# Five experts kept on chip in place of three, Y loaded three pieces sooner, and a last expert of 32 slots

## The chip, the cores and the metric

The kernel runs on one core of one Trainium2 chip. Its time is device microseconds of one execution; before the change the median of 3 runs is 979.84 us (975.59 to 984.9). The engines of the core are PE (TensorE, matmuls), VectorE (DVE in the rows), ScalarE (ACT), GpSimd (POOL) and SyncE (SP). Loads and stores are issued on SyncE's queue in program order; gathers and scatters by row index are issued by POOL.

## What is computed

One block over 512 tokens of width 1024: a convolution branch and a gated spatial branch, mixed and projected, then a mixture of 32 experts in 4 groups, and a last RMS norm. The part that the change touches is the end:

```python
e_w = jax.nn.softmax(top_v, axis=-1) * g_w          # two experts for each token
def run_block(args):
    xb, e = args
    return (jax.nn.silu(xb @ w_gate[e]) * (xb @ w_up[e])) @ w_down[e]
...
x = x + hierarchical_moe(h, ...)                    # sum of the two experts' rows, weighted
return rms_norm(x, norm_final_g)
```

Each expert has weights of 3 x 2 MB (gate and up in two halves of the contraction, and down), 201 MB in all, in float32. 512 tokens with two experts each make 1024 assignments.

## The kernel before

**Order of the experts.** The experts are ranked by their number of tokens (`kr`), except that ranks 0 to 2 are three fixed experts, whose weights can be loaded before the routing is known. Ranks 3 to 7 get 128 slots ("b"), 8 to 17 get 64 ("s"), 18 to 31 get 32 ("t"); ranks 0 to 2 also 64. The string `ORDER` (line 24) says in which order these are run, after the three fixed ones. In this text "expert n" is the n-th in that order, 0 to 31, and not a rank. Before, experts 27 to 31 are "s".

**The stream of weights.** `loads` (lines 772 to 776) lists the pieces in order of loading: (n, 0) and (n, 1) are the two halves of gate and up of expert n, (n, 2) its down weights, 2 MB each; (n - 1, 2) comes behind (n, 1). ("Y", 0) and ("Y", 1) are pieces too, 2 MB each. `piece()` (line 809) issues the next one on SyncE's queue; a weight piece waits until the piece two before it in turn has landed (`DEEP`, `throttle`), and each waits until its tile is free. There are nine tiles of 2 MB used in turn; one of them leaves the turn when ("late", 0) comes and holds tables from then on. The last expert's pieces are cut in 2, 4 and 4 DMAs. A DMA that waits holds up everything behind it on SyncE's queue.

**One expert.** POOL gathers its token rows; PE transposes them (`x_tr`, line 949). `up` (lines 967 and 971) makes gate and up, `glu` (978, 983) the product on ScalarE and VectorE, `h_tr` (990, 992) its transposes, and `down` (1001, 1013) the output. Experts of 64 slots run two column groups of 64 on PE, those of 32 slots four groups of 32. The main loop is software pipelined: `up(n, 0)`, `up(n, 1)`, `glu(n)`, `x_tr(n + 1)`, `down(n - 1)`, `h_tr(n)`. The program is scheduled by hand: each engine runs in the order in which the code is written.

**Where outputs go.** The output rows of experts 0 to 28 are scattered by POOL to the DRAM buffer `yd` (lines 1017 and 1039); its two halves, the first and the second choice of each token, are loaded as Y0 and Y1 (line 821), weighted and added to X by VectorE (`y_add`, line 1130). Y0's load waits for the scatters, and `scattered` (line 1156) holds it back in the program until they are issued. The last `NLATE` = 3 experts are not scattered. Experts 29 and 30 leave their rows side by side in one tile `LT["c"]` (`late_down`), and `late_add` multiplies it with a one-hot matrix that holds the weights (`late_oh`), so that PE puts each row at its token, and VectorE adds it to X (lines 1123 and 1125, 8 matmuls and 8 additions).

**The end.** The last expert's tokens get their whole row of X on PE as well: its slots' rows of X are picked by matmuls with `LT["ot"]` (`late_x`, line 1180) into the accumulator in which its down matmuls add (1001). For the other rows `finish_a` (1134, squares), `rsqrt` and `finish_b` (1138, product; 1139, store) make the final norm. The last expert's rows are normed at lines 1200 to 1204 and scattered over the output at line 1205.

Of the kernel before, what the change touches and what calls it, by code (L numbers as in the profile page):

```python
# [10 lines left out]
I32 = mybir.dt.int32  # L11
# [10 lines left out]
NS, NBIG, DEEP, NLATE, LATE_AT = 3, 8, 2, 3, -16  # L22
NOV, NMID = 15, 18
ORDER = "tsb" * 5 + "t" * 9 + "s" * 5
# [57 lines left out]
def body(tc, nc, d, out, dbg=None):  # L82
# [692 lines left out]
    loads = loads[:-3] + [(NE - 2, 2), ("Y", 0), ("Y", 1)] + [(NE - 1, q) for q in range(3)]  # L775
# [272 lines left out]
    sv, so = kt_([2, 2], "sv"), kt_([1], "so", I32)  # L1048
    mx, over = kt_([1], "mx"), kt_([1], "over", I32)

    def route_rest():
        for q in range(NLATE):
            r, h = order[NE - NLATE + q], (slice(0, 64), slice(64, 128), slice(0, 128))[q]
            dve.tensor_copy(sv[h, q // 2, 0:1], tb1[h, r:r + 1])
        dve.tensor_scalar(sv[:, :, 1], sv[:, :, 0], -float(T), None, ALU.add)
        dve.tensor_scalar(so, gi[:, order[-1]:order[-1] + 1], 2.0, hf01, ALU.mult, ALU.add)
# [16 lines left out]
        dve.tensor_tensor(same.rearrange("p (q s) -> p q s", q=2), ident[:, :64].unsqueeze(1).to_broadcast([128, 2, 64]),  # L1073
                          ident[:, 64:].unsqueeze(1).to_broadcast([128, 2, 64]), ALU.add)

    def late():
# [3 lines left out]
        LT["oh"] = t[:, D:D + T]  # L1080
# [13 lines left out]
    def late_oh(q):  # L1094
        last = q == 1
        oh = LT["tm"] if last else LT["oh"]
# [47 lines left out]
    for n in range(NE - 1):  # L1144
# [222 lines left out]
```

## Time and profile before

| | |
|---|---|
| median of 3 runs | 979.84 us (975.59 to 984.9) |
| profiled execution, its own time | 978.58 us |
| its span | 976.7 us |
| PE, VectorE, ScalarE, POOL busy | 88%, 42%, 22%, 10% of the span |
| data moved by DMA | 270.18 MB |

The execution shown in the rows below is the profiled one. The span runs from the first to the last instruction of the program; the time of an execution is some 1.9 us longer here. Matmuls in float32 have two records each in the trace, so 8 matmuls stand as x16.

### The profile page before, as it was taken

Reading aid. Unit: us, or ns where it says so; the run is one execution under the profiler, and the core shown is the slowest. Engines: PE = TensorE matmul, PEld = TensorE weight load, DVE = VectorE, ACT = ScalarE, POOL = GpSimd, SP = SyncE. Lnnn points to the kernel's source line nnn. Section 1 sums busy time; section 2 is a strip of 40 time slices with the busy share of each in tenths; the row PEclk is TensorE's granted clock in tenths of the full one; section 3 lists DMA queues with packets and bytes.
Section 4 is the critical chain, followed back from the end, with each engine's and each line's share of the span. In section 5 each row is a group of like instructions: output and inputs, shape, how many; then the busy total and the mean of one; then the engine's idle time right before and its main releaser. Section 6 shows DMA issues by size and latency. Waiting matters only on the chain.

```text
span 976.7 us, 11811 instructions
## 1 busy us (share of the span) xinstructions
PE 855.3 (88%) x4774; PEld 542.3 (56%) x4774; DVE 408.4 (42%) x715; ACT 219.0 (22%) x317; POOL 98.2 (10%) x97
## 2 busy tenths in 40 slices
PE   8999899999999999997599999797978765667883
PEld 6886578888877888886234443343433332322231
DVE  7796958888987633426401110010101000003063
ACT  6221222433216623233211101010101000001022
POOL 2220000000000000320211111010101111100000
PEclk9999999999999999999799999899999677789997
DMA  6538422222222232697599999999999999999994
GB/s 229 194 101 287 136 81 87 87 87 87 87 87 87 86 117 99 260 407 289 197 395 397 415 422 407 387 416 401 403 405 416 411 419 406 413 406 427 430 414 184
DMA packets 36253, 270.18 MB, mean 277 GB/s; under 512 B 7044, under 2 KB 9864, under 8 KB 19682
## 3 DMA queue, kind: packets, MB, share of 16 engines
q1 hardware_dynamic: 30912, 259.09, 66.8%
q0 software_dynamic: 5280, 10.28, 2.9%
q8 instruction: 39, 0.64, 0.3%
q14 instruction: 20, 0.16, 0.1%
q10 hardware_dynamic: 2, 0.00, 0.0%
HBM read 258.56 MB, written 15.73 MB: 281 GB/s over the span
## 4 chain that ended last, share of the span: by engine, by line
PE 44%; DMA 40%; DVE 8%; issue 3%; ACT 2%; SPq 1%; POOL 1%; POOLq 0%; DVEq 0%; ACTq 0%
DMA w<-in_wexp 37%; PE acc L357 22%; PE acc L365 7%; PE acc L971 7%; DVE cv L347 3%; PE acc L1001 3%; DMA f<-in_wmix 2%; DVE hl L169 1%; PE acc L336 1%; POOL hl L171 1%; ACT hl L158 1%; PE acc L967 1%; PE aux L478 1%; SPq L329 1%; PE acc L669 1%
## 5 line engine op out<-in xcount | busy, mean ns | idle before, releaser
L357 PE MATMUL acc<-hT,hl 128*128 128x512 f32 x912 | 211.7, 392 | 0.0
L971 PE MATMUL acc<-w,xT 128*64 128x512 f32 (+1 forms) x576 | 173.5, 620 | 23.8 <-DMA w<-in_wexp 22.9
L357 PEld LDWEIGHTS acc<-hT,hl 128*128 128x128 f32 x912 | 171.5, 189 | 37.0 <-issue 1.8
L983 DVE TENSOR_TENSOR h<-sg,acc 64x256 f32<-64x256 f32 (+2 forms) x31 | 17.4, 560 | 363.8 <-ACT sg L978 268.4
L971 PEld LDWEIGHTS acc<-w,xT 128*64 128x64 f32 (+1 forms) x576 | 61.3, 158 | 122.1 <-issue 101.7
L347 DVE SCALAR_TENSOR_TENSOR cv<-cv,cs,cv 128x500 f32<-128x500 f32 (+16 forms) x180 | 124.9, 752 | 0.6
L169 DVE TENSOR_TENSOR hl<-f,hl 128x2048 fp32r<-128x2048 f32 (+1 forms) x36 | 80.4, 2234 | 60.5 <-ACT hl L158 60.4
L967 PE MATMUL acc<-w,xT 128*32 128x256 f32 x896 | 66.2, 451 | 32.5 <-DMA w<-in_wexp 32.5
L1001 PE MATMUL acc<-w,hh 128*64 128x512 f32 (+1 forms) x288 | 83.1, 598 | 7.9 <-DMA w<-in_wexp 6.1
L158 ACT ACTIVATE hl<-f 128x2048 fp32r<-128x2048 f32 x35 | 66.8, 1912 | 61.2 <-issue 29.2
L978 ACT ACTIVATE sg<-acc 64x256 f32<-64x256 f32 (+2 forms) x32 | 16.0, 501 | 259.0 <-PE acc L971 167.1
L967 PEld LDWEIGHTS acc<-w,xT 128*32 128x32 f32 x896 | 32.0, 126 | 60.4 <-issue 24.9
L1001 PEld LDWEIGHTS acc<-w,hh 128*64 128x64 f32 (+1 forms) x288 | 29.2, 151 | 47.8 <-issue 41.1
L889 POOL DMA_INDIRECT xg<-h2d,gi x32 | 30.6, 956 | 234.4 <-PE aux L949 226.8
L1013 PE MATMUL acc<-w,hh 128*32 128x256 f32 x448 | 34.7, 463 | 17.5 <-DMA w<-in_wexp 17.5
L365 PE MATMUL acc<-hl,mT 128*128 128x512 f32 x192 | 47.0, 396 | 0.0
L614 POOL TENSOR_TENSOR X<-X,rbo 128x1024 f32<-128x1024 f32 x4 | 9.4, 2395 | 350.6 <-DVE hl L169 350.6
L357 PE MATMUL acc<-yT,hl 128*128 128x512 f32 x192 | 44.2, 389 | 0.0
L357 PE MATMUL acc<-sT,hl 128*128 128x512 f32 x192 | 44.2, 389 | 0.0
L365 PE MATMUL acc<-hl,hT 128*128 128x512 f32 x192 | 43.8, 390 | 0.0
L365 PEld LDWEIGHTS acc<-hl,hT 128*128 128x128 f32 x192 | 36.0, 188 | 8.3 <-issue 0.8
L357 PEld LDWEIGHTS acc<-sT,hl 128*128 128x128 f32 x192 | 36.1, 188 | 7.5
(274 smaller groups left out, 711.6 us busy)
## 6 DMA issues: line engine op xcount, KB each, us to landing
w<-in_wexp SPq DMA_DIRECT2D x93, 2048.0 KB, 10.5
f<-in_wmix SPq DMA_DIRECT2D x36, 1024.0 KB, 4.8
yd<-z SPq DMA_DIRECT2D x1, 4096.0 KB, 13.5
w<-yd SPq DMA_DIRECT2D x2, 2048.0 KB, 13.9
w<-in_wexp SPq DMA_DIRECT2D x8, 512.0 KB, 10.9
xs<-in_x SPq DMA_DIRECT2D x4, 512.0 KB, 5.9
X<-in_x SPq DMA_DIRECT2D x4, 512.0 KB, 6.1
h2d<-h POOLq DMA_DIRECT2D x4, 512.0 KB, 7.5
```

What stands on the lines that cost most here:

```text
L158: act.activation(HI[i], src, AF.Copy)
L169: dve.tensor_tensor(LO[i][:, :n], src[:, :n], h[:, :n], ALU.subtract)
L347: dve.scalar_tensor_tensor(cY[:, j, s_:], cA[:, j, :T - s_], cw(j, t), cY[:, j, s_:], ALU.mult, ALU.add)
L357: pe.matmul(p, w[:, k], mv[m][:, k], start=n == 0, stop=n == 3 * KT - 1)
L365: pe.matmul(p, mv[m][:, kh * 4 + k, bs], w[:, k], start=kh + n == 0, stop=kh == 1 and n == 11)
L889: pool.indirect_dma_start(out=XG[n % len(XG)][:m], out_offset=None, in_=h2d, in_offset=bass.IndirectOffsetOnAxis(ap=gi[:m, r:r + 1], axis= ...
L967: pe.matmul(E[n]["p"][i * 32:i * 32 + 32, :256], XT[n][:, kt], w[:, 1 - i // 2, kk, f:f + 256], start=kt == 0, stop=kt == KT - 1, skip_gro ...
L971: pe.matmul(E[n]["gu"[q]], XT[n][:, kt], w[:, q, kk], start=kt == 0, stop=kt == KT - 1, skip_group_check=True)
L978: act.activation(s_, E[n]["g"], AF.Silu)
L983: dve.tensor_tensor(h, s_, E[n]["u"], ALU.mult)
L1001: pe.matmul(y[hf], E[n]["hT"][:, kt], w[:, kt, hf * 512:hf * 512 + 512], start=first and kt == 0, stop=kt == 3, skip_group_check=True)
L1013: pe.matmul(p[i * 32:i * 32 + 32, :256], E[n]["hT"][:, kt % 2, f:f + 32], w[:, kt, i * 256:i * 256 + 256], start=kt == 0, stop=kt == 3, sk ...
```

## The change

`ORDER` puts one "t" behind the five "s", so that experts 26 to 30 have 64 slots and expert 31 has 32. `NLATE` becomes 5: experts 27 and 28 are kept in one tile, 29 and 30 in another, and `pair_add` adds each pair to X; the scatters end with expert 26. The tables for this need another one-hot matrix and are made two iterations sooner (`LATE_AT`, `late_rows`, `late_oh`). The Y pieces stand ahead of (30, 0). The eight Y additions move into the loop's last iteration, and the first pair's additions into the last two. The last expert runs in four groups of 32 slots, with 256 columns each, its X rows are taken between the two halves of `up`, and its output rows are scattered in quarters of a row.

```diff
-NS, NBIG, DEEP, NLATE, LATE_AT = 3, 8, 2, 3, -16
+NS, NBIG, DEEP, NLATE, LATE_AT = 3, 8, 2, 5, -22
-ORDER = "tsb" * 5 + "t" * 9 + "s" * 5
+ORDER = "tsb" * 5 + "t" * 8 + "s" * 5 + "t"
...
-    loads = loads[:-3] + [(NE - 2, 2), ("Y", 0), ("Y", 1)] + [(NE - 1, q) for q in range(3)]
+    loads = loads[:-3] + [(NE - 2, 2)] + [(NE - 1, q) for q in range(3)]
+    loads[-7:-7] = [("Y", 0), ("Y", 1)]
     loads.insert(LATE_AT, ("late", 0))
...
     def late_down(n, y):
-        if n == NE - NLATE:
-            LT["c"] = m1.tile([128, 2, DE], F32, name="yc", tag="ysb", bufs=2)
+        q, i = divmod(n - NE + NLATE, 2)
+        if i == 0:
+            LT["c", q] = m1.tile([128, 2, DE], F32, name="yc", tag="ysb", bufs=2)
...
+    def pair_add(q, bs=range(NB)):
+        for b in bs:
+            late_add([LT["oh"][:, q]] * 2, [LT["c", q][:, hf] for hf in range(2)], b)
+
+    def last_down(p, first):
+        w = W[NE - 1, 2].rearrange("p (k f) -> p k f", k=4)
+        for kt in range(4):
+            f = kt // 2 * 32
+            for i in range(4):
+                pe.matmul(p[i * 32:i * 32 + 32, :256], E[NE - 1]["hT"][:, kt % 2, f:f + 32], w[:, kt, i * 256:i * 256 + 256],
+                          start=first and kt == 0, stop=kt == 3, skip_group_check=True)
...
         x_tr(n + 1)
+        if n == NE - 2:
+            Y = [W["Y", j] for j in range(2)]
+            for b in range(NB):
+                y_add(Y, 0, [b])
+                y_add(Y, 1, [b])
         if n:
             down(n - 1)
+            if n == NE - NLATE:
+                scattered.append(True)
             piece()
-        if n == NE - NLATE:
-            scattered.append(True)
         h_tr(n)
...
+        if n in (NE - 3, NE - 2):
+            pair_add(0, (0, 1) if n == NE - 3 else (2, 3))
...
     down(NE - 2)
-    for b in range(NB):
-        y_add(Y, 0, [b])
-        late_add([LT["oh"]] * 2, [LT["c"][:, hf] for hf in range(2)], b)
...
+    for b in range(NB):
+        pair_add(1, (b,))
+        finish_a(O, [b])
+    rsqrt(fs[:, 1], fs[:, 0], fs[:, 2], 1.0 / D)
+    act.activation(f1[:, 0:1], eps, AF.Silu)
+    up(NE - 1, 0)
...
+    p = acc()
+    for b in range(NB):
+        for i in range(4):
+            pe.matmul(p[i * 32:i * 32 + 32, :256], LT["ot"][:, b, :32], X2[:, b, i * 256:i * 256 + 256], start=b == 0,
+                      stop=False, skip_group_check=True)
+    up(NE - 1, 1)
+    finish_b(O, (0, 1))
+    glu(NE - 1)
+    h_tr(NE - 1)
+    finish_b(O, (2, 3))
+    act.activation(f1[:, 0:1], eps, AF.Sqrt)
+    last_down(p, False)
```

On SyncE's queue, the loads near the end before (`w92` is (29, 2), `w93` is (30, 2), `w94` and `w95` are Y0 and Y1, `w96` the first half of expert 31; the number behind a w is the place in the list of pieces):

```order
L836 DMA w92_5509<-in_wexp 128x4096
L836 ISA
L836 DMA w93_5519<-in_wexp 128x4096
L821 DMA w94_5631<-yd_75 128x4x1024
L821 DMA w95_5641<-yd_75 128x4x1024
L828 TENSOR_LOAD eid_3250
L836 ISA
L836 DMA w96_5670<-in_wexp 128x2x1024
```

and after the change (`w89` is (28, 2), `w90` and `w91` are Y0 and Y1, `w92` and `w93` the halves of expert 30, `w94` is (29, 2), `w95` is (30, 2)):

```order
L837 DMA w89_5430<-in_wexp 128x4096
L822 DMA w90_5469<-yd_75 128x4x1024
L822 DMA w91_5499<-yd_75 128x4x1024
L829 TENSOR_LOAD eid_3250
L837 ISA
L837 DMA w92_5509<-in_wexp 128x4096
L837 ISA
L837 DMA w93_5541<-in_wexp 128x4096
L837 ISA
L837 DMA w94_5559<-in_wexp 128x4096
L837 ISA
L837 DMA w95_5569<-in_wexp 128x4096
```

The Y loads have moved from places 94 and 95 to 90 and 91; both halves of expert 30 and both down pieces behind them come two places later.

On PE, the end of the program before, from the down matmuls of expert 29 on (`yc` is the tile of kept rows, `X` the residual, `same` the matrix that sums the squares of a row's parts):

```order
L1001 MATMUL acc<-w_5509,hh 64x512 x8
L990 MATMUL acc<-ident,h 128x64 x4
L1001 MATMUL acc<-w_5519,hh 64x512 x8
L1123 MATMUL acc<-yc,w_5225 128x512 x8
L971 MATMUL acc<-w_5670,xT 64x512 x8
L971 MATMUL acc<-w_5683,xT 64x512 x8
L1180 MATMUL acc<-X_2744,w_5225 64x512 x8
L990 MATMUL acc<-ident,h 128x64 x4
L1001 MATMUL acc<-w_5688,hh 64x512 x8
L1202 MATMUL aux<-cs,same 128x1
```

and after the change, from the same matmuls on:

```order
L1002 MATMUL acc<-w_5559,hh 64x512 x8
L991 MATMUL acc<-ident,h 128x64 x4
L1136 MATMUL acc<-yc,w_5053 128x512 x4
L1002 MATMUL acc<-w_5569,hh 64x512 x8
L1136 MATMUL acc<-yc,w_5053 128x512 x8
L968 MATMUL acc<-w_5597,xT 32x256 x16
L1199 MATMUL acc<-X_2744,w_5053 32x256 x16
L968 MATMUL acc<-w_5631,xT 32x256 x16
L991 MATMUL acc<-ident,h 128x64 x2
L1130 MATMUL acc<-w_5644,hh 32x256 x16
L1211 MATMUL aux<-cs,same 128x1
```

Four more additions of kept rows stand between the last two 64-slot down products, the X rows stand ahead of the second half of `up`, and the last expert's matmuls are of 32 rows and 256 columns.

On VectorE, the same stretch before (`w_5631` is Y0, `w_5641` Y1; h is the product of `glu`):

```order
L983 TENSOR_TENSOR h<-sg,acc 64x512
L952 TENSOR_TENSOR xT<-aux,gfp 128x512
L1130 SCALAR_TENSOR_TENSOR X_2744<-w_5631,wt,X_2744 128x1024
L1125 TENSOR_TENSOR X_2744<-X_2744,acc 128x512 x2
```

which goes on so for the other three token blocks, then the four additions of Y1 and the norm. After the change, from the product of expert 30 on:

```order
L984 TENSOR_TENSOR h<-sg,acc 64x512
L953 TENSOR_TENSOR xT<-aux,gfp 128x256
L1143 SCALAR_TENSOR_TENSOR X_2744<-w_5469,wt,X_2744 128x1024
L1143 SCALAR_TENSOR_TENSOR X_2744<-w_5499,wt,X_2744 128x1024
```

again four times in turn, then this:

```order
L1138 TENSOR_TENSOR X_2744<-X_2744,acc 128x512 x12
L120 TENSOR_SCALAR fs<-fs 128x4
L121 RECIPROCAL fs<-fs 128x4
L122 SCALAR_TENSOR_TENSOR fs<-fs 128x4
L123 TENSOR_TENSOR fs<-fs 128x4
L124 SCALAR_TENSOR_TENSOR fs<-fs 128x4
L1151 SCALAR_TENSOR_TENSOR w_5703<-X_2744,fs,w_5053 128x1024 x2
L982 SCALAR_TENSOR_TENSOR h<-sg,cs,acc 64x256
L1151 SCALAR_TENSOR_TENSOR w_5703<-X_2744,fs,w_5053 128x1024 x2
```

All eight Y additions now stand directly behind expert 30's product and ahead of the pair additions, and two output rows' products stand ahead of the last expert's `h`.

## Rows read from the trace of the kernel before

**Rows 1.** From the page: the span, the DMA digits and rates in 40 slices of 24.4 us, and the chain that ended last by engine and by line.

```profile
span 976.7 us, 11811 instructions
...
DMA  6538422222222232697599999999999999999994
GB/s 229 194 101 287 136 81 87 87 87 87 87 87 87 86 117 99 260 407 289 197 395 397 415 422 407 387 416 401 403 405 416 411 419 406 413 406 427 430 414 184
...
PE 44%; DMA 40%; DVE 8%; issue 3%; ACT 2%; SPq 1%; POOL 1%; POOLq 0%; DVEq 0%; ACTq 0%
DMA w<-in_wexp 37%; PE acc L357 22%; PE acc L365 7%; PE acc L971 7%; DVE cv L347 3%; PE acc L1001 3%; DMA f<-in_wmix 2%; DVE hl L169 1%; PE acc L336 1%; POOL hl L171 1%; ACT hl L158 1%; PE acc L967 1%; PE aux L478 1%; SPq L329 1%; PE acc L669 1%
```

**Rows 2.** Timeline of PE near the end: start, busy time, line, operation, tiles, count, and in brackets the idle time before it and what ended that. L971 is `up`, L1001 a down, L990 transposes, L1123 the addition of kept experts, L1180 the last expert's X rows.

```profile
913.47 3.65 PE L1001 MATMUL acc<-w,hh 128*64 128x512 f32 x16 [0.77 <-DMA w<-in_wexp]
917.05 0.46 PE L990 MATMUL acc<-ident,h 64*128 64x64 f32 x4
918.30 3.65 PE L971 MATMUL acc<-w,xT 128*64 128x512 f32 x16 [0.80 <-DMA w<-in_wexp]
923.26 3.65 PE L971 MATMUL acc<-w,xT 128*64 128x512 f32 x16 [1.30 <-DMA w<-in_wexp]
...
928.32 3.65 PE L1001 MATMUL acc<-w,hh 128*64 128x512 f32 x16 [0.76 <-DMA w<-in_wexp]
...
933.67 3.65 PE L1001 MATMUL acc<-w,hh 128*64 128x512 f32 x16 [1.31 <-ACT hh L992]
938.01 7.13 PE L1123 MATMUL acc<-yc,w 128*128 128x512 f32 x16 [0.69 <-ACT yc L1117]
...
954.11 3.60 PE L1180 MATMUL acc<-X,w 128*64 128x512 f32 x16
```

**Rows 3.** Busy time of each engine in four stretches near the end: microseconds from the span's start, length, then busy time and count of instructions by engine, granted clock, DMA share and GB/s.

```profile
920.00:930.00 10.00, 7.93 (x42) 2.90 (x40) 1.28 (x2) 0.59 (x1) 0.00 (x0) 1.00 1.01 431
...
940.00:950.00 10.00, 9.05 (x30) 3.28 (x31) 9.69 (x13) 0.26 (x2) 0.00 (x0) 1.00 1.03 417
950.00:960.00 10.00, 9.10 (x44) 2.64 (x42) 8.61 (x13) 8.33 (x14) 0.00 (x0) 1.00 1.03 403
960.00:970.00 10.00, 2.61 (x14) 0.79 (x10) 3.38 (x11) 1.08 (x4) 0.98 (x1) 0.78 0.36 141
```

**Rows 4.** The chain of waits from 893 us on, in order of time: start, length, what.

```profile
893.67 9.57 DMA w<-in_wexp
...
923.34 9.79 DMA w<-in_wexp
...
937.87 15.29 DMA w<-in_wexp
...
953.20 1.08 PE acc L971 x4
...
958.57 3.68 PE acc L1001 x16
...
966.06 0.71 POOL out L1205
```

**Rows 5.** Timeline of the same stretch, VectorE's Y additions (L1130), pair additions (L1125) and output rows (L1138), and one of ScalarE's squares (L1134).

```profile
938.17 1.28 DVE L1130 SCALAR_TENSOR_TENSOR X<-w,wt,X 128x1024 f32<-128x1024 f32 x1 [9.30 <-DMA w<-yd]
...
939.56 1.28 DVE L1125 TENSOR_TENSOR X<-X,acc 128x512 f32<-128x512 f32 x2
...
948.52 4.86 DVE L1130 SCALAR_TENSOR_TENSOR X<-w,wt,X 128x1024 f32<-128x1024 f32 x4
...
949.83 1.06 ACT L1134 ACTIVATE w<-X 128x1024 f32<-128x1024 f32 x1 [9.74 <-DVE X L1130]
...
956.40 2.47 DVE L1138 SCALAR_TENSOR_TENSOR w<-X,fs,w 128x1024 f32<-128x1024 f32 x2
```

**Rows 6.** Two rows of PE's timeline, each one piece of a 32-slot expert, and, below them, groups by line and shape over 560 to 977 us: count, busy time, mean ns of one, idle time before.

```profile
856.83 3.37 PE L967 MATMUL acc<-w,xT 128*32 128x256 f32 x32 [2.33 <-DMA w<-in_wexp]
861.84 1.93 PE L967 MATMUL acc<-w,xT 128*32 128x256 f32 x32 [1.65 <-DMA w<-in_wexp]
...
L952 DVE TENSOR_TENSOR xT<-aux,gfp 128x512 f32<-128x512 f32 x16 | 10.5, 674 | 0.0
L952 DVE TENSOR_TENSOR xT<-aux,gfp 128x256 f32<-128x256 f32 x12 | 5.0, 416 | 0.3 <-PE aux L949 0.2
...
L983 DVE TENSOR_TENSOR h<-sg,acc 64x256 f32<-64x256 f32 x12 | 4.9, 412 | 138.7 <-ACT sg L978 138.7
...
L978 ACT ACTIVATE sg<-acc 64x256 f32<-64x256 f32 x12 | 4.6, 380 | 85.8 <-PE acc L967 85.8
...
L992 ACT ACTIVATE hh<-acc 128x128 f32<-128x128 f32 x13 | 3.6, 277 | 3.0 <-PE acc L990 2.9
```

**Rows 7.** Two stretches of the 32-slot experts, columns as in rows 3.

```profile
856.40:859.80 3.40, 2.97 (x28) 1.36 (x32) 0.00 (x0) 0.00 (x0) 0.00 (x0) 0.50 0.98 379
859.80:866.60 6.80, 2.97 (x48) 1.51 (x40) 1.87 (x6) 0.38 (x1) 0.97 (x1) 1.00 1.00 427
```

**Rows 8.** Y's wait for the scatters in SyncE's queue (total, times, longest), the down matmuls of expert 26 on PE's timeline, and the times from issue to landing of the scatters of line 1039.

```profile
SPq L821 <- DMA yd<-ysb,si: 2.6, 1, 2.6
...
883.94 1.93 PE L1013 MATMUL acc<-w,hh 128*32 128x256 f32 x32 [1.85 <-DMA w<-in_wexp]
...
DMA to landing us min/median/max: 8.1/8.9/11.0
```

More of the change, by code (lines that the diff above doesn't have):

```diff
@@ L1072, in route_rest @@
         dve.tensor_tensor(wt[:, 3], wt[:, 2], wt[:, 0], ALU.mult)
-        dve.tensor_tensor(same.rearrange("p (q s) -> p q s", q=2), ident[:, :64].unsqueeze(1).to_broadcast([128, 2, 64]),
-                          ident[:, 64:].unsqueeze(1).to_broadcast([128, 2, 64]), ALU.add)
+        dve.tensor_copy(same.rearrange("p (q s) -> p q s", q=4), sel.unsqueeze(1).to_broadcast([128, 4, 32]))
     def late():
@@ L1094, in late_oh @@
     def late_oh(q):
-        last = q == 1
-        oh = LT["tm"] if last else LT["oh"]
+        last = q == NLATE // 2
+        oh = LT["tm"] if last else LT["oh"][:, q]
         tm = LT["o1"] if last else LT["tm"]
@@ L1170, in body @@
-    act.activation(f1[:, 0:1], eps, AF.Sqrt)
-    up(NE - 1, 0)
-    for hf in range(2):
-        sp.dma_start(LT["tm"][hf * 64:hf * 64 + 64],
-                     bass.AP(tensor=rows.tensor, offset=rows.offset + R_GN + hf * 512, ap=[[0, 64], [1, 512]]))
-    p = acc()
-    y = [p[:64], p[64:]]
-    def late_x(b):
-        for hf in range(2):
-            pe.matmul(y[hf], LT["ot"][:, b], X2[:, b, hf * 512:hf * 512 + 512], start=b == 0, stop=False,
-                      skip_group_check=True)
@@ L1183, in body @@
-    for b in range(NB):
-        y_add(Y, 1, [b])
-        if b < 3:
-            finish_a(O, [b])
-    rsqrt(fs[:, 1, :3], fs[:, 0, :3], fs[:, 2, :3], 1.0 / D)
-    finish_b(O, (0,))
-    up(NE - 1, 1)
-    glu(NE - 1)
-    finish_a(O, [3])
-    for b in range(NB):
-        late_x(b)
-    h_tr(NE - 1)
-    finish_b(O, (1, 2))
-    rsqrt(fs[:, 1, 3:], fs[:, 0, 3:], fs[:, 2, 3:], 1.0 / D)
-    finish_b(O, (3,))
-    down_mm(NE - 1, y, False)
-    o31 = m1.tile([128, DE], F32, name="o31", tag="ysb", bufs=2)
@@ L1200, in body @@
-    act.activation(o31, p, AF.Square, accum_out=f1[:, 0:1])
+        pair_add(1, (b,))
[4 more added lines that the diff above has]
+    for i in range(4):
+        sp.dma_start(LT["tm"][i * 32:i * 32 + 32, :256],
+                     bass.AP(tensor=rows.tensor, offset=rows.offset + R_GN + i * 256, ap=[[0, 32], [1, 256]]))
+    p = acc()
+    for b in range(NB):
+        for i in range(4):
+            pe.matmul(p[i * 32:i * 32 + 32, :256], LT["ot"][:, b, :32], X2[:, b, i * 256:i * 256 + 256], start=b == 0,
+                      stop=False, skip_group_check=True)
@@ L1201, in body @@
+    up(NE - 1, 1)
[3 more added lines that the diff above has]
+    finish_b(O, (2, 3))
+    act.activation(f1[:, 0:1], eps, AF.Sqrt)
+    last_down(p, False)
+    o31 = m1.tile([128, 256], F32, name="o31", tag="ysb", bufs=2)
+    act.activation(o31, p[:, :256], AF.Square, accum_out=f1[:, 0:1])
     q = aux()
```

41 lines of the change are left out of this document (22 added, 19 removed).

## The prediction

> **What bounds the kernel now.** I read the page first. Its DMA digits stand at 9 from about 590 us to the end at some 400 to 430 GB/s, and the chain of work that ended last puts 37% of the span on the loads of expert weights [rows 1]. So from there on the kernel is a stream of 2 MB pieces, one each 4.95 us (the PE's waits for pieces end at 913.47, 918.30, 923.26 and 928.32 [rows 2]), and the span is the time at which the stream ends, plus what is left to do then. A gain must come from fewer bytes or from a shorter tail.
>
> Next the windows of the last 60 us: DMA share about 1.0 up to 960, 0.36 in 960 to 970 [rows 3]. The chain of waits shows the tail: the last piece on it, a quarter of the last expert's second half, lands at 953.16; then come four matmuls of `up`, the X rows of the last expert (3.60 us), its down matmuls from 958.57, and the closing scatter, issued by 966.77 [rows 2, 4]. The last expert's third piece is not on that chain: at the spacing it lands by about 958.1, while PE begins to need it at 958.57.
>
> Before the tail, PE and VectorE were busy together: PE added the pair of kept experts in 7.13 us from 938.01 [rows 2], VectorE added Y and the pair to X from 938.17, when Y had landed, to 953.38 [rows 5]. That this ends within a microsecond of the last second-half piece (953.16) means that loads, PE and VectorE are about level there: taking work from one of them alone gives little.
>
> **The change, part by part.** Landing times here are those of the execution shown, whose time is 978.58 us for a span of 976.7; the median of the runs shown is 979.84, 1.3 above.
>
> *Bytes.* Five experts' outputs are no longer scattered in place of three, and the smallest is among them. The 1024 assignments over 32 experts make 32 rows of 4 KB on average, 128 KB; the two more experts hold at most 64 and 32 rows. At 430 GB/s [rows 3] the full 96 rows are 0.9 us, two experts of half the average 0.3; I take 0.5, an average expert and one of about half. Y itself stays 4 MB, and the pieces are as many as before. The last expert's norm row falls from 256 to 128 KB behind the last piece: hidden, the stream is over by then.
>
> *Positions in the stream.* The two Y pieces go ahead of expert 30's gate and up. Expert 30's halves move from the places that landed at 918.2 and 923.2 to those that landed at 928.2 and 933.1; expert 29's down piece moves from the place of 928.2 to that of Y0, 938.1 [rows 2, 4, 5]. With the 0.5 saved: expert 30's second half 932.6, 29's down 937.6, 30's down 942.6, the last expert at 947.5, 952.6 and 957.6. That is the other side of loading Y sooner: PE gets its last big experts some 10 us later, and the work that hangs on them moves with it.
>
> *PE from 937.7.* The order is down(29), transposes, half a pair's additions, down(30), the second pair's additions, `up` of the last expert's first half, its X rows, second half. Each is in the rows: 3.65 for a down; 0.46 for four transposes; 8 additions 7.13, so 4 are 3.57 [rows 2]. Thus 937.7 + 3.65 + 0.46 + 3.57 + 3.65 = 949.0. The first addition waited 0.69 for ScalarE's copy [rows 2]; the second pair then runs 949.7 to 956.9. A piece of a 32-slot expert is 1.93 us [rows 6]: up(31,0) to 958.8. The X rows were 3.60 for 64 slots [rows 2]; the 32-slot form does not occur before. The bounds are 3.60 and the 1.93 of the same count of 32-row matmuls; I take 1.93, since it has that shape. So to 960.7, and up's second half to 962.6; its piece landed at 952.6 and is no longer waited for. Silu 0.38 and the product 0.41 [rows 6] with small gaps, two transposes about 0.35, a copy 0.28 [rows 6], down 1.93: the last down ends about 966.3. Before, it ended at 958.57 + 3.65 = 962.2 [rows 2]. That is 4.1 later. From there the chain is the same with half the width: Square and the last product on 256 in place of 512 columns save about 0.26 each (0.674 against 0.416 for such a VectorE pair [rows 6]). **Sum: 4.1 - 0.5 = 3.6 us later.**
>
> *What lies beside it.* VectorE gets 8 Y additions after expert 30's product: half 30,1 from 932.7, up 3.65, Silu and product about 1.4, xT 0.42: start 938.1. Eight at 4.86/4 = 1.215 [rows 5] end at 947.8, four pair additions at 0.64 [rows 5] at 950.4, before PE's second pair gives more. Then it follows PE and ends 957.5. Behind that come ScalarE's last Square (1.06 + about 0.2 [rows 5]), a square root and five small VectorE operations (about 1.1 together), and the first two output rows (2.47 [rows 5]), all of them ahead of the last expert's product on VectorE: done at about 962.4, against 963.0 when Silu is. That cover is 0.6 us; if PE were faster by more, this queue would set the same end. So whatever else the 32-slot expert saves on PE is worth little while VectorE's queue stands there.
>
> *The gate on the last piece.* It reuses Y0's tile and so waits, in SyncE's queue, for the seventh Y addition, 938.1 + 8.5 = 946.6. The piece ahead lands at 952.6, so the engines still have 6 us of work queued: no cost. The output rows, behind it in that queue, come at 961 or later. The tile taken 6 pieces sooner for the late tables leaves eight tiles in turn; a tile returns after at least six pieces (30 us), and a piece's work is 2 to 4 us: no cost. The pair additions at n = 29 fall into PE's hole while Y loads (917.5 to 927.8): no cost, and without that hole 3.57 us.
>
> **The clock.** In that hole PE idles about 6 us behind the pair additions. Rows of the same program show both levels: in 856.4 to 859.8 the granted clock is 0.50, the 1.2 GHz level, and 32 matmuls that take 1.93 at 2.4 GHz take 3.37 [rows 6, 7], after a stretch with idle time between pieces. So expert 30's first half may run at the low level. With one such stretch of 3.4 us it takes 1.7 more and ends at 933.1, the second half at 936.8, and the wait for 29's down at 937.6 takes that up; at the low level throughout it would take 7.3 from 927.8, the second half would end at 938.7, and down(29) would start 1 us late. I count nothing and keep that 1 us for the range. If a low stretch falls after 937.7, each 3.4 us of it costs 1.7. The Trainium skill, "TensorE: Matmul & The Clock Gate", section "Part 1: The HAM clock gate (the 'warmup' mystery)", says that half rate is the default and that sustained activity lifts it, which speaks against a change that opens a hole for PE just ahead of its longest run. The trace agrees as far as it shows both levels (0.50 and 1.00); by that rule the sum would be 3.6 to 4.6, by the row 3.6.
>
> **The rivals.**
> *The stream still sets the end* (the tail gets shorter). For it: 37% of the chain are these loads [rows 1], and the last expert's own chain is shorter by half. Then down ends 0.5 after the last piece, 957.6 + 0.6 = 958.2 in place of 962.2; with the 0.5 from the width: 4.5 faster, 974.1. Against it: PE's sum, which has hardly a free place from 937.7 on; it would have to lose 8 us.
> *The clock falls in the tail.* Around VectorE's waits PE has gaps there. One or two low stretches: 1.7 to 3.4 more, 984 to 986.
> *Slower by over 1%: Y0 blocks SyncE's queue.* Y0's load waits for the scatter of every expert not kept, now expert 26's, and all weights are queued behind it. Before, this wait was 2.6 us [rows 8]. Expert 26's down can begin at about 884 [rows 8], its scatter is issued by 889 and takes 8.1 to 11.0 [rows 8]: landed by 900. SyncE comes to Y0 when the piece that landed at 903.2 is in, and the two behind it are in flight until 913.3 [rows 2, 4]. So the stream starves only from a scatter landing after 913.3, each microsecond costs one from there, and it needs some 6 more beside the 3.6 for 1%. 13 us of margin speak against it.
>
> **How the numbers follow.** PE's later chain 0.72; the stream sets the end 0.10; the clock 0.12; the blocked queue 0.02; the other 0.04 is a stream that differs in rate as a whole. The sum gives 978.58 + 3.6 = 982.2 on this execution's scale and 983.4 on the median's; I forecast 983.0. The unknown X rows add up to 1.7, the hole's clock 1, the bytes take 0.4 either way. With the stream rival below (974.1, or 975.4 on the median's scale) and the clock above (986, 987.3), and the spread of the runs themselves (975.59 to 984.9), the range is 976 to 989. About 1%, 9.8 us, is what a measurement of this kernel can tell from no change: only the blocked queue, or a stream of another rate, reaches it upward, and downward nothing in the tail can, since the end cannot come before the last piece. Faster by over 1% 0.03, within 0.91, slower 0.06.
>
> **What would show it.** Right: down(29) starts near 937.7; the second pair's additions run without a wait for a piece, 949.7 to 957; up's second half waits for PE's order and not for a load; the last down ends near 966, some 8 us after its piece; Y0's issue shows no wait; the chain of waits shows PE and VectorE, not DMA, in the last 25 us. Wrong: PE waiting for the last expert's pieces (then the tail got shorter), Y additions starting much before 938, or a hole in the DMA share between 900 and 958.

## The result

| | before | after |
|---|---|---|
| median, 20 runs each on one chip | 981.46 us (974.99 to 988.03) | 987.55 us (979.3 to 993.02) |
| profiled execution, its span | 978.58 us, 976.7 | 987.66 us, 985.2 |
| data moved by DMA | 270.18 MB | 269.83 MB |

The ratio is 1.0051 [1.0034, 1.0069]: some 5.0 us slower, between 3.3 and 6.8 on 981.46. The forecast was 3.6 us slower by the sum, as a time 983.0 us in a range of 976 to 989: 987.55 lies inside it. Of the distance to 983.0, 1.6 us come from the median before, which was 979.84 in the 3 runs that the forecast was built on and 981.46 in these 20.

The two profiled executions can't be laid on each other from the start: the stream of pieces runs up to a few us sooner or later in each execution. A common mark helps, the issue of place 89, (28, 2), on SyncE's queue. It is the last piece ahead of those that the change moves; the expectations below mean this same issue where they say place 88. SyncE's timeline before:

```profile
903.36 0.33 SPq L836 DMA_DIRECT2D w<-in_wexp  x1
```

and after:

```profile
906.76 0.33 SPq L837 DMA_DIRECT2D w<-in_wexp  x1
```

From the mark to the end of the span were 73.35 us before (976.71 - 903.36) and are 78.45 after (985.21 - 906.76), 5.1 more. That agrees with the measured 5.0, so I look for the loss behind the mark; the 3.4 us by which the mark itself lies later are within its spread (in the executions below it lies between 899.9 and 914.1, in kernels that differ little ahead of it). One execution of the kernel before can't show a small shift of the mark itself; but pair_in_hole and y_split below have everything ahead of the mark from the changed kernel, and their ratios are 1.0005 and 1.0006, which leaves little for that part. Below, "at +x" means x us behind the mark.

PE's timeline of the kernel after, which answers to [rows 2]; L972 is `up`, L1002 a down, L1136 the pairs' additions, L968 `up` of the 32-slot expert, L1199 its X rows, L1130 its down:

```profile
923.22 3.70 PE L1136 MATMUL acc<-yc,w 128*128 128x512 f32 x8 [0.30 <-ACT yc L1118]
932.70 9.09 PE L972 MATMUL acc<-w,xT 128*64 128x512 f32 x32 [5.78 <-DMA w<-in_wexp]
...
942.47 3.65 PE L1002 MATMUL acc<-w,hh 128*64 128x512 f32 x16
...
946.45 3.70 PE L1136 MATMUL acc<-yc,w 128*128 128x512 f32 x8
950.08 3.65 PE L1002 MATMUL acc<-w,hh 128*64 128x512 f32 x16
954.42 7.13 PE L1136 MATMUL acc<-yc,w 128*128 128x512 f32 x16 [0.69 <-ACT yc L1118]
961.49 1.93 PE L968 MATMUL acc<-w,xT 128*32 128x256 f32 x32
963.24 1.91 PE L1199 MATMUL acc<-X,w 128*32 128x256 f32 x32
964.96 1.91 PE L968 MATMUL acc<-w,xT 128*32 128x256 f32 x32
967.88 0.33 PE L991 MATMUL acc<-ident,h 64*128 64x64 f32 x2 [1.01 <-DVE h L982]
968.58 1.93 PE L1130 MATMUL acc<-w,hh 128*32 128x256 f32 x32 [0.37 <-ACT hh L993]
```

Behind expert 30's `up` at 932.70 no row shows a wait for a load: PE runs through, in the order that the prediction wrote down. (That down(29) starts just as its piece lands is taken up further down.) The hole is the 5.78 us ahead of expert 30's `up`.

The windows of the same stretch (columns as in [rows 3]):

```profile
920.00:930.00 10.00, 6.62 (x24) 2.34 (x20) 3.00 (x5) 1.56 (x3) 0.00 (x0) 1.00 1.04 436
930.00:940.00 10.00, 7.30 (x26) 2.58 (x28) 0.00 (x0) 0.00 (x0) 0.00 (x0) 0.66 1.01 423
940.00:950.00 10.00, 9.92 (x46) 3.94 (x42) 7.44 (x8) 2.17 (x4) 0.00 (x0) 1.00 0.96 359
950.00:960.00 10.00, 9.31 (x30) 3.63 (x30) 9.29 (x13) 4.93 (x8) 0.00 (x0) 1.00 1.04 403
960.00:970.00 10.00, 8.63 (x130) 4.50 (x132) 7.91 (x13) 6.22 (x12) 0.00 (x0) 1.00 0.49 193
```

The granted clock fell in the hole (0.66 over 930 to 940), so the 32 records of expert 30's `up` took 9.09 us in place of 7.3, and was 1.00 from 940 to the last down. The DMA share stays at 0.96 or more to 960, while PE worked 14 us of the 20 from 920 to 940.

VectorE's timeline, which answers to [rows 5] (L1143 Y additions, L1138 pair additions, L1151 output rows, L982 the last expert's product h, L1213 the last product of the program):

```profile
943.39 10.14 DVE L1143 SCALAR_TENSOR_TENSOR X<-w,wt,X 128x1024 f32<-128x1024 f32 x8
...
961.60 0.69 DVE L1138 TENSOR_TENSOR X<-X,acc 128x512 f32<-128x512 f32 x1 [0.17 <-PE acc L1136]
...
964.75 2.48 DVE L1151 SCALAR_TENSOR_TENSOR w<-X,fs,w 128x1024 f32<-128x1024 f32 x2 [0.15 <-DVE fs L124]
967.36 0.47 DVE L982 SCALAR_TENSOR_TENSOR h<-sg,cs,acc 64x256 f32<-64x256 f32 x1
...
972.92 0.48 DVE L1213 SCALAR_TENSOR_TENSOR o<-acc,cs,w 128x256 f32<-128x256 f32 x1 [0.22 <-DVE cs L124]
```

The pair additions follow PE one by one (0.17 us of waiting each) to the end of X at 962.28.

The end of the chain of waits, which answers to the last row of [rows 4] (in this trace the chain goes back no further than its first row here):

```profile
973.99 0.03 POOLq L1214
...
975.08 0.70 POOL out L1214
```

and the rows of the closing scatter's own line, POOL's semaphore waits and the DMA:

```profile
L1214 POOLq EVENT_SEMAPHORE  x2: 43/43/43, 972.8 to 974.0; - x2
...
L1214 POOL DMA_INDIRECT out<-o,cs x1: 992/992/992, 974.8 to 974.8; - x1
```

The product that the scatter sends is done at 973.40 (972.92 + 0.48). Yet POOL's last wait ends at 974.0 and the scatter starts at 974.79, 1.39 us after the product; before it started 0.28 us after it (product done at 965.51, scatter at 965.79). Something else than the product let it go.

### The profile page after: what moved, and what is told of

It reads as the page before. It is cut to its first block, busy times and chain, and to the rows that moved or that the text cites. A ratio compares the mean times of both kernels' runs of the same rounds, so it can differ in the third digit from the quotient of the medians.

```text
span 985.2 us, 11884 instructions
## 1 busy us (share of the span) xinstructions
PE 862.7 (88%) x4806; PEld 546.6 (55%) x4806; DVE 415.1 (42%) x723; ACT 220.6 (22%) x320; POOL 96.5 (10%) x95
## 2 busy tenths in 40 slices
DMA packets 36127, 269.83 MB, mean 274 GB/s; under 512 B 6975, under 2 KB 9923, under 8 KB 19555
## 5 line engine op out<-in xcount | busy, mean ns | idle before, releaser
L972 PE MATMUL acc<-w,xT 128*64 128x512 f32 (+1 forms) x576 | 180.4, 653 | 27.8 <-DMA w<-in_wexp 27.0
L984 DVE TENSOR_TENSOR h<-sg,acc 64x512 f32<-64x512 f32 (+2 forms) x31 | 17.6, 569 | 365.9 <-ACT sg L979 271.5
L972 PEld LDWEIGHTS acc<-w,xT 128*64 128x64 f32 (+1 forms) x576 | 64.1, 165 | 130.0 <-issue 120.3
L968 PE MATMUL acc<-w,xT 128*32 128x256 f32 x896 | 62.6, 432 | 27.9 <-DMA w<-in_wexp 27.9
L1002 PE MATMUL acc<-w,hh 128*64 128x512 f32 (+1 forms) x288 | 83.0, 598 | 4.5 <-DMA w<-in_wexp 4.4
L968 PEld LDWEIGHTS acc<-w,xT 128*32 128x32 f32 x896 | 30.7, 121 | 54.7 <-DMA w<-in_wexp 23.5
L1002 PEld LDWEIGHTS acc<-w,hh 128*64 128x64 f32 (+1 forms) x288 | 29.0, 151 | 45.1 <-issue 42.0
L1014 PE MATMUL acc<-w,hh 128*32 128x256 f32 x416 | 31.9, 458 | 17.9 <-DMA w<-in_wexp 17.9
## 6 DMA issues: line engine op xcount, KB each, us to landing
w<-in_wexp SPq DMA_DIRECT2D x93, 2048.0 KB, 10.7
```

Of the source, the lines that this page charges most:

```text
L968: pe.matmul(E[n]["p"][i * 32:i * 32 + 32, :256], XT[n][:, kt], w[:, 1 - i // 2, kk, f:f + 256], start=kt == 0, stop=kt == KT - 1, skip_gro ...
L972: pe.matmul(E[n]["gu"[q]], XT[n][:, kt], w[:, q, kk], start=kt == 0, stop=kt == KT - 1, skip_group_check=True)
L984: dve.tensor_tensor(h, s_, E[n]["u"], ALU.mult)
L1002: pe.matmul(y[hf], E[n]["hT"][:, kt], w[:, kt, hf * 512:hf * 512 + 512], start=first and kt == 0, stop=kt == 3, skip_group_check=True)
L1014: pe.matmul(p[i * 32:i * 32 + 32, :256], E[n]["hT"][:, kt % 2, f:f + 32], w[:, kt, i * 256:i * 256 + 256], start=kt == 0, stop=kt == 3, sk ...
```

## The experiments

**Theory A**: PE's order sets the end. Behind expert 29's down piece PE has work without a gap, and what stands there in excess is half a pair's additions and a hole ahead of it that could have held them. **The rivals**: the clock that fell in the hole delays PE; VectorE's eight Y additions, put together behind expert 30's product, set the end (**theory D**). **Theory E** is about the last 1.1 us: the scatter writes into the output, as the four stores of the norm's rows do, and waits until these have landed. It has to: they write the rows of the last expert's tokens too, without that expert's part.

Ends of the last product, start of the scatter and end of the span, from the mark on, worked out from each trace as above:

| kernel | ratio to before | product done | scatter | end |
|---|---|---|---|---|
| before | | 62.15 | 62.43 | 73.35 |
| after | 1.0051 [1.0034, 1.0069] | 66.64 | 68.03 | 78.45 |
| y_late | 1.0022 [0.9989, 1.0056] | 65.09 | 65.70 | 76.36 |
| pair_in_hole | 1.0005 [0.9976, 1.0035] | 63.59 | 63.90 | 74.44 |
| yadd_in_hole | 1.0045 [1.0015, 1.0075] | 66.10 | 67.44 | 77.80 |
| both_in_hole | 1.0023 [0.999, 1.0056] | 63.39 | 64.73 | 76.12 |
| half_rows | one run | 66.63 | 66.91 | 77.69 |
| busy_hole | one run | 65.93 | 66.23 | 76.96 |
| y_split | 1.0006 [0.998, 1.0032] | 62.10 | 62.43 | 73.02 |
| last64 | 1.0112 [1.0075, 1.015] | 76.07 | 76.35 | 86.82 |
| split_row0 | 1.0025 [0.9999, 1.0051] | 60.56 | 63.62 | 74.52 |
| split_h | 1.0029 [1.0006, 1.0052] | 59.65 | 63.92 | 74.31 |

**pair_in_hole** moves the second half of the first pair's additions from behind down(29) into the hole.

```diff
-        if n in (NE - 3, NE - 2):
-            pair_add(0, (0, 1) if n == NE - 3 else (2, 3))
+        if n == NE - 3:
+            pair_add(0)
```

> The changed kernel, but the first pair is added for all four token blocks in the iteration of expert 29, in the hole that PE has while Y loads, and not half there and half between down(29) and down(30). Same work in all. Theory A (PE's chain from down(29) on is gapless and sets the end): PE loses 3.6 us of it, so the second pair's additions, the last expert and the closing scatter all come 3.0 to 3.7 us earlier; 1.001 to 1.002 of the kernel before. Theory B (the amount of work): no change, 1.005. Theory C (the stream with Y in its new place runs slower and sets the end): no change, 1.005.

PE's timeline of it:

```profile
934.80 3.65 PE L1002 MATMUL acc<-w,hh 128*64 128x512 f32 x16 [0.62 <-DMA w<-in_wexp]
...
940.15 3.65 PE L1002 MATMUL acc<-w,hh 128*64 128x512 f32 x16 [1.30 <-ACT hh L993]
944.49 7.13 PE L1136 MATMUL acc<-yc,w 128*128 128x512 f32 x16 [0.69 <-ACT yc L1118]
```

From down(29) to the second pair are 9.69 us (944.49 - 934.80) in place of 11.95 (954.42 - 942.47), and everything behind moves with it: X is done 3.0 us earlier, the product 3.05. The edit itself makes 2.26 of this, since 1.30 us of the place that it frees go into a wait for ScalarE ahead of down(30); the other 0.8 is down(29)'s own start, +34.92 in place of +35.71, which followed its piece. So the expected 3.0 to 3.7 was met by the number, but not by the edit alone. The scatter gains 4.1, since the stores were in before the product here; half_rows below comes back to them. By the ratios, 1.0005 [0.9976, 1.0035] against 1.0051 [1.0034, 1.0069], Theory A has the larger part of the loss. The rivals B and C of the expectation fall: the work and the order of the stream are those of the changed kernel, the time is not.

**yadd_in_hole** moves the eight Y additions instead, into the hole on VectorE; the pair's halves stay as after the change. **both_in_hole** does both.

```diff
-        if n == NE - 2:
-            Y = [W["Y", j] for j in range(2)]
-            for b in range(NB):
-                y_add(Y, 0, [b])
-                y_add(Y, 1, [b])
...
+        if n == NE - 3:
+            Y = [W["Y", j] for j in range(2)]
+            for b in range(NB):
+                y_add(Y, 0, [b])
+                y_add(Y, 1, [b])
```

> The changed kernel, but the eight Y additions stand at the end of the iteration of expert 29, ahead of expert 30's product on VectorE, where VectorE is idle. Theory A (PE sets the end, VectorE has a microsecond or so of cover): 0 to 0.7 us less, 1.004 to 1.005 of the kernel before; the Y additions run from about 928 us on and VectorE waits for PE afterwards. Theory D (VectorE's queue of Y additions behind expert 30's product sets the end): 3 us or more less.

> The changed kernel with the first pair's additions and the eight Y additions both in the iteration of expert 29. Theory A: PE's 3.6 us and nothing more, as with the pair alone: 3.0 to 4.3 us less than the changed kernel, 1.000 to 1.002 of the kernel before, since PE still has down(30), a pair's additions and the last expert behind the piece (30, 2). Theory D: clearly more than with the pair alone, 6 us or more less than the changed kernel.

With the Y additions gone the product ends 0.54 us earlier than after the change, and down(29) already starts 0.54 earlier there (+35.17), ahead of all that was moved; with both moved, 0.20 earlier than with the pair alone. Theory D falls: VectorE's Y queue had room beside PE. In both the scatter is again 1.3 us behind the product.

**busy_hole** fills the hole with seven matmuls more, whose result nothing reads, so that PE's clock does not fall.

```diff
+            if n == NE - 3:
+                p = aux()
+                for b in range(7):
+                    pe.matmul(p, LT["oh"][:, 0, :128], LT["c", 0][:, 0], start=True, stop=True)
```

> The changed kernel with seven more 128x128 by 512 matmuls (their result is not used) behind the first pair's additions in the iteration of expert 29, about 6 us that fill PE's hole. Theory A: the granted clock stays at 1.00 there and expert 30's two halves take 7.1 to 7.4 us of PE in place of 9.09, but down(29) still starts when its piece lands and the chain from there is as long: 0 to 0.7 us less from the place 88 of the stream to the last product. Rival (the clock's fall in the hole costs the time): 1.5 to 2.5 us less.

PE's timeline, then the window that held the hole:

```profile
930.50 3.65 PE L972 MATMUL acc<-w,xT 128*64 128x512 f32 x16 [0.62 <-DMA w<-in_wexp]
935.33 3.65 PE L972 MATMUL acc<-w,xT 128*64 128x512 f32 x16 [1.17 <-DMA w<-in_wexp]
...
940.27 3.65 PE L1002 MATMUL acc<-w,hh 128*64 128x512 f32 x16 [0.67 <-DMA w<-in_wexp]
```

```profile
930.00:940.00 10.00, 7.92 (x40) 2.89 (x40) 0.34 (x1) 0.59 (x1) 0.00 (x0) 1.00 1.01 433
```

The clock is 1.00, both halves of `up` take 3.65, and down(29) waits for its piece: it starts at +35.0 (940.27 - 905.27) in place of +35.7 after the change. The product is done 0.71 earlier. But expert 30's `up`, which waited for its piece in both, already began 0.71 earlier here, at +25.23 (930.50 - 905.27) against +25.94 (932.70 - 906.76), so the 0.71 is the stream's and not the clock's. What the fall of the clock adds to `up` (9.09 against 7.3) is hidden where the piece of down(29) lands later still. The clock as the cause of the whole falls.

**half_rows** leaves out the output rows of token blocks 2 and 3 (their products and their stores), so that half of the output rows are not written by them.

```diff
-    finish_b(O, (2, 3))
```

> The changed kernel without the final norm's product and store of token blocks 2 and 3 (their output rows are left out). Theory E (the closing scatter writes the output tensor and so waits for the stores of the output rows, the last of which land after VectorE's last product): without the two last stores POOL issues the scatter 0.2 to 0.4 us after VectorE's last product in place of 1.39. Rival (POOL is late for another reason, such as its own sequencer): 1.2 to 1.5 as before. The rest of the chain, from the place 88 of the stream to that product, as in the changed kernel within 0.7 us.

The product is done at +66.63, as after the change to 0.01, and POOL's timeline says

```profile
980.99 0.99 POOL L1213 DMA_INDIRECT out<-o,cs  x1 [81.55 <-DVE o L1212]
```

released by the product, 0.28 us behind it, as expected. By itself that is no proof: in pair_in_hole and busy_hole, with all four stores, the scatter came 0.31 and 0.30 behind the product. The times from issue to landing of the stores decide it, after the change:

```profile
L1152 SPq DMA_DIRECT2D out<-w x4: 332/345/369, 966.1 to 970.2; - x4
...
DMA to landing us min/median/max: 3.7/3.7/3.7
```

and in busy_hole:

```profile
L1152 SPq DMA_DIRECT2D out<-w x4: 332/344/366, 963.9 to 968.0; - x4
...
DMA to landing us min/median/max: 2.6/2.6/2.7
```

After the change the last store, issued at 970.2, landed at 973.9, and POOL's wait ended at 974.0. In busy_hole it landed at 970.6, ahead of the product (971.19), which then let the scatter go. both_in_hole agrees (965.8 + 3.7, the wait ends at 969.5). Theory E holds: the stores held the scatter for 1.11 us (1.39 - 0.28) in the execution shown. But that is no cost of the change. The last store is issued 3.2 us ahead of the product in it and in busy_hole, and was issued 3.3 ahead before (962.25 and 965.51); what differs is how long it took to land.

**y_late** puts the Y pieces back to where they stood, between (29, 2) and expert 31, and the Y additions back among the pair additions; five experts kept and a 32-slot last expert remain.

```diff
-    loads = loads[:-3] + [(NE - 2, 2)] + [(NE - 1, q) for q in range(3)]
-    loads[-7:-7] = [("Y", 0), ("Y", 1)]
+    loads = loads[:-3] + [(NE - 2, 2), ("Y", 0), ("Y", 1)] + [(NE - 1, q) for q in range(3)]
...
```

> All of the change, but Y0 and Y1 back at their old place behind (30, 2), and the Y additions back behind down(30). Theory A (the places in the stream set it: expert 29's and 30's down pieces come two places later, and PE's gapless chain behind them ends later): PE's down(29) and down(30) move some 10 us forward again, VectorE ends its additions to X about where the kernel before does, and the end is then set by the output rows, their stores, and the closing scatter that waits for those stores; I expect 4 to 6 us less than the changed kernel, 0.996 to 1.001 of the kernel before. Theory B (the work of two more kept experts costs the time wherever Y lies): 1.004 to 1.006 of the kernel before, as changed.

That missed: the end came 2.1 us earlier from the mark and not 4 to 6, and the ratio tells neither theory from the other. The big experts are early again (down(29) at +25.72), but PE's timeline shows what else stands there:

```profile
933.31 3.70 PE L1135 MATMUL acc<-yc,w 128*128 128x512 f32 x8
936.94 3.65 PE L1001 MATMUL acc<-w,hh 128*64 128x512 f32 x16
941.29 7.13 PE L1135 MATMUL acc<-yc,w 128*128 128x512 f32 x16 [0.69 <-ACT yc L1117]
...
953.00 4.23 PE L1197 MATMUL acc<-X,w 128*32 128x256 f32 x32 [2.72 <-DVE X L1142]
...
961.92 0.33 PE L990 MATMUL acc<-ident,h 64*128 64x64 f32 x2 [2.96 <-DVE h L981]
962.62 3.21 PE L1129 MATMUL acc<-w,hh 128*32 128x256 f32 x32 [0.37 <-ACT hh L992]
```

Without the hole the pair's halves have no free place on PE: the second pair begins at 941.29, before the change at 938.01 [rows 2] (the marks are 903.62 and 903.36). VectorE, which adds Y and pair in turn, ends X 2.9 us later from the mark, and the X rows and the last product h wait for it.

**y_split** combines: Y0 at the place ahead of (30, 2), Y1 behind it, the first pair wholly ahead of down(29), Y0's additions in the last iteration, Y1's among the second pair's.

```diff
-    loads[-7:-7] = [("Y", 0), ("Y", 1)]
+    loads[-4:-4] = [("Y", 0)]
+    loads[-3:-3] = [("Y", 1)]
...
-            for b in range(NB):
-                y_add(Y, 0, [b])
-                y_add(Y, 1, [b])
+            y_add(Y, 0)
...
+        y_add(Y, 1, [b])
         pair_add(1, (b,))
```

> A version built on Theory A: the places of (30, 0), (30, 1) and (29, 2) as in the kernel before, then Y0, (30, 2), Y1 and the last expert; the first pair's additions wholly in the iteration of expert 29, Y0's additions behind expert 30's product, Y1's among the second pair's. Expert 30's down comes one place later than in the kernel before and one sooner than in the changed one, PE has 3.6 us less behind it than in the changed kernel, and VectorE splits its Y additions. Theory A: additions to X end 49.5 to 51 us behind the start of place 88 (50.0 before, 55.5 changed), and the end is 0.5 to 3 us ahead of the kernel before: 0.997 to 0.9995. Theory B (the work of two more kept experts costs the time wherever it lies): 1.003 to 1.005.

X is done at +49.64, 0.4 earlier than before the change; the gain is gone two rows on. VectorE's timeline, then PE's:

```profile
958.23 2.48 DVE L1152 SCALAR_TENSOR_TENSOR w<-X,fs,w 128x1024 f32<-128x1024 f32 x2 [0.15 <-DMA w<-in_wexp]
960.63 0.47 DVE L983 SCALAR_TENSOR_TENSOR h<-sg,cs,acc 64x256 f32<-64x256 f32 x1
```

```profile
961.15 0.34 PE L992 MATMUL acc<-ident,h 64*128 64x64 f32 x2 [2.98 <-DVE h L983]
961.86 3.47 PE L1131 MATMUL acc<-w,hh 128*32 128x256 f32 x32 [0.37 <-ACT hh L994]
```

h stands behind the norm of all four blocks and two output rows, PE idles 2.98 us for it, and the down of the 32-slot expert then takes 3.47 in place of 1.93, hardly less than 64 slots did before (3.65 [rows 2]).

**split_row0 and split_h** are y_split with one and with no output row ahead of h. The edit of split_row0 against y_split:

```diff
-    finish_b(O, (0, 1))
+    finish_b(O, (0,))
     glu(NE - 1)
     h_tr(NE - 1)
-    finish_b(O, (2, 3))
+    finish_b(O, (1, 2, 3))
```

> As y_split, but only one output row's product stands ahead of the last expert's h on VectorE, the other three behind it. If VectorE's queue (the norm of four blocks and two output rows) is what held h in y_split, then h begins about 1.2 us earlier after the issue of place 88 than there (53.3 in place of 54.5), the last product ends about 60.9 in place of 62.1, and if the clock's fall in the last down (3.47 us for 32 slots) came from PE's wait of 2.98 us for h, the down is shorter too, down to 1.93, and the product ends near 59.4. Ratio to before 0.997 to 0.999. The rival, that h waits for something else (up's last piece, Silu), has all these times as in y_split and a ratio of 1.000.

> As y_split, but the last expert's h stands ahead of all four output rows on VectorE. By the same theory h begins when Silu is done, 1.7 to 2.4 us earlier than in y_split (52.1 to 52.8 after the issue of place 88), and the last product ends 59.7 to 60.4, or near 58.2 if the down's clock stays high; but the last output row is not earlier than in y_split, so the closing scatter may now wait for its store, which lands some 2.6 to 3.5 us after the last row's product: scatter at 60.5 to 62 in place of 62.4. Ratio to before 0.997 to 1.000. Rival as in split_row0: no change against y_split.

Both ratios missed (1.0025 and 1.0029; the table has the intervals). The product moves as expected: done at +60.56 and +59.65, the down at 1.93 us again. In split_row0 h itself starts no sooner from the mark (+54.52, X being done 1.2 later there), so that part of its expectation was not put to the test. But the scatter comes at +63.62 and +63.92, later than in y_split. Its line in split_row0:

```profile
L1214 POOLq EVENT_SEMAPHORE  x2: 43/43/43, 963.3 to 964.5; - x2
...
L1214 POOL DMA_INDIRECT out<-o,cs x1: 992/992/992, 965.3 to 965.3; - x1
```

The product is done at 962.24, and POOL waits until 964.5 for the stores: the scatter is now 3.06 us behind the product (4.27 in split_h). The end of X, the norm, four rows and their stores are a second chain to the scatter, about as long as PE's; in these executions, whose stores took 4.2 and up to 4.8 us to land, shortening PE's beyond y_split brought nothing. No version here is faster than the kernel before by what can be measured.

**last64** takes only the 32 slots back: the last expert has 64, as before, and its tail the width of before.

```diff
-ORDER = "tsb" * 5 + "t" * 8 + "s" * 5 + "t"
+ORDER = "tsb" * 5 + "t" * 9 + "s" * 5
```

> The changed kernel with the old order of experts: 31 has 64 slots again and runs as in the kernel before (two column groups, X rows of 64 slots), all the rest as changed. Theory A (PE's chain sets the end): up's halves, X rows and down take 3.65, 3.6, 3.65 and 3.65 us in place of four times 1.93: 6 to 7.5 us more than the changed kernel, 1.011 to 1.013 of the kernel before. Rival (what the prediction said of VectorE's queue: the 32 slots save PE time where VectorE holds the last expert anyway): 0 to 2.5 more, 1.005 to 1.0075.

PE's timeline, then the row of h on VectorE's:

```profile
956.33 3.65 PE L972 MATMUL acc<-w,xT 128*64 128x512 f32 x16
959.81 3.60 PE L1201 MATMUL acc<-X,w 128*64 128x512 f32 x16
963.24 3.60 PE L972 MATMUL acc<-w,xT 128*64 128x512 f32 x16
...
969.25 5.35 PE L1002 MATMUL acc<-w,hh 128*64 128x512 f32 x16 [0.47 <-ACT hh L993]
```

```profile
967.52 0.74 DVE L982 SCALAR_TENSOR_TENSOR h<-sg,cs,acc 64x512 f32<-64x512 f32 x1 [5.46 <-ACT sg L979]
```

h starts 5.14 us later from the mark than after the change (+65.74 against +60.60), which is what three rows of 32 slots save on PE (1.72 + 1.69 + 1.69); the down adds 3.4, of which 1.7 are by the lower clock (0.68 over 969.2 to 974.6; 5.35 against the 3.65 of such a down before [rows 2]). Of the three parts of the change the 32 slots are the only one that was shown to gain, some 6 us by the ratios ((1.0112 - 1.0051) x 981.3), and 8.4 from the mark in the execution shown.

## Why the prediction was right, and where it was off

**What held.** PE's order from down(29) on, with every duration: half a pair 3.70 (3.57 forecast), down 3.65, ScalarE's copy 0.69, pair 7.13, `up` 1.93, X rows 1.91 (the lower bound, 1.93, was taken). From the start of down(29) to the end of the last down the sum said 28.6 us; 28.04 were measured (942.47 to 970.51). `up`'s second half waited for PE, not for a load. The last two rows of half the width saved 0.40 us (2.89 against 3.29 from the end of the down to the end of the product; forecast 0.5). The gate on the last piece and Y0's place in SyncE's queue cost nothing that reached the end. The step that named the price of loading Y sooner, the last big experts 10 us later, is what pair_in_hole and y_split bear out: with the pair's half out of PE's way, or Y later, most of the 5 us is gone.

**What was mis-sized.** The step "29's down 937.6" put down(29) at +34.3 (937.7 - 903.36); it started at +35.7. Its piece set that. SyncE issues a piece when the one two places before it has landed, the Y pieces not counted, so its issues tell the landings of (28, 2) and of (29, 2) after the change:

```profile
918.02 0.35 SPq L837 DMA_DIRECT2D w<-in_wexp  x1
...
942.46 0.70 SPq L837 DMA_DIRECT2D w<-in_wexp  x1
```

(29, 2) landed at +35.7 (942.46 - 906.76), and down(29) started then; PE had been done with what stands ahead of it at 942.40. In the six other executions that have Y0 and Y1 in this place the piece landed at +34.5 to +35.2, nearer to the forecast. The lag of this execution stands ahead of the hole: (28, 2) landed at +11.3 (918.02 - 906.76), in the other eleven at +9.8 to +10.7.

The clock's fall, which the sum had as 0 with 1 us kept for the range, cost less than 0.1 us here. In half_rows it cost more, as its piece was early; SyncE's issue on the landing of (29, 2), then down(29):

```profile
948.99 0.70 SPq L837 DMA_DIRECT2D w<-in_wexp  x1
```

```profile
949.78 3.65 PE L1002 MATMUL acc<-w,hh 128*64 128x512 f32 x16
```

Expert 30's `up` took 10.02 us there, and down(29) began 0.8 us behind its piece; in last64 it took 10.08 and the delay was 1.0. In yadd_in_hole it took 8.47 and PE still waited 0.69 for the piece. So 1 us for the range was the right size. The trace agrees with the sentence of the Trainium skill that was weighed there ("TensorE: Matmul & The Clock Gate", Part 1) as far as the granted clock did fall in the hole, 0.66 in that window. The last down ended 4.9 us later from the mark than before (63.75 against 58.86), forecast 4.1.

**What was missed.** The sum went from the last product straight to the scatter, as before. That the scatter also waits for the stores of the output rows was not in it; the prediction had looked at these stores only as something that comes "at 961 or later" behind the last piece in SyncE's queue. In the two executions laid side by side the sum of all is +4.9 for the last down, -0.4 for the width, +1.1 for the stores, and 0.5 less from the scatter to the end (10.42 us against 10.92): 5.1. The last two terms are not owed to the change: the stores had the same lead as before, and from the scatter to the end it was 10.36 to 11.39 us over all executions. What is owed to it shows in the last product. In after, half_rows, yadd_in_hole and busy_hole, which run the same work from down(29) to that product but for Y's additions, it was done at +65.93 to +66.64 against +62.15 before, 3.8 to 4.5 us later, where the sum said 3.6 and the runs 3.3 to 6.8.

**One remark misled.** "Whatever else the 32-slot expert saves on PE is worth little while VectorE's queue stands there" holds only for savings beyond those counted: VectorE's rows ended at 967.23, right when h could start at 967.36. The savings that were counted lie fully on the path, as last64 shows. The cover of 0.6 us forecast for that queue was 0.1; in y_split, where PE is earlier, it is gone and the queue costs what was feared.

**The rivals.** The stream did not set the end (behind down(29) no row waits for a load), Y0 did not block SyncE's queue, and the clock stayed at 1.00 in the tail of the changed kernel; it fell there in y_late, y_split and last64. The saved bytes, 0.35 MB and 0.8 us at 430 GB/s, were not tested by themselves. Nor was a kernel that keeps three experts with only Y moved, so what five in place of three bring alone stays open. Two readings were off without bearing on the sum: the DMA digits stand at 9 from about 488 us (20 slices of 24.4), not 590, and the sign that the chain of waits would show PE and VectorE can't be read, since the chain of this trace begins at the scatter's wait.

## What to carry to other kernels

When a transfer is moved forward in a stream that is full, ask which pieces move back by as much, and what work hangs on the last of them; the hole that it opens is only worth something if work from behind is moved into it. A closing scatter into a tensor that other stores write too ends two chains, its own data and the landing of those stores: put both in the sum, and find which ends last after each edit. A later chain made shorter shows at once what stood just beside it: VectorE's norm here, and behind that the stores.

## What the runs showed of the hardware

Stores of 512 KB (one output row block) landed 2.6 to 4.8 us after their issue, which decides the scatter's start when the last store and the last product are close. The same four stores at the same distance from the product took 3.7 us after the change and 2.6 to 2.7 in busy_hole.

The same 32 records of the last down took 1.93 us where PE had idled 1.01 to 1.78 us ahead of the transposes before it (after, split_h, split_row0) and 3.21 and 3.47 where it had idled 2.96 and 2.98 (y_late, y_split); the 64-slot form took 5.35 after 1.47 us (last64). The granted clock over these downs was 1.00 in the first three and 0.64, 0.65 and 0.68 in the others. Ahead of expert 30's `up` PE idled 3.20 us in pair_in_hole and 3.21 in both_in_hole behind the same additions of the pair; the clock over `up` was 0.83 in the one (8.53 us) and 1.00 in the other (twice 3.65). So the idle time alone does not tell when the clock falls.

In the window 940 to 950 after the change the DMA share stayed at 0.96 while the rate was 359 GB/s, against 403 to 436 around it. No experiment was made on it; PE waited for no piece there.
